# Text order on three engines for the last four pairs of the first half, the scheduler's order ahead of them

## The chip, the cores and the metric

The kernel runs on one core of one Trainium2 chip. The metric is the device time of one execution in microseconds (us). The engines are TensorE (PE in the profile, with its weight loads as PEld), VectorE (DVE), ScalarE (ACT), GpSimd (POOL) and SyncE (SP); SP issues most of the DMAs.

## What is computed

One block of an encoder on a sequence of 2048 tokens with 1024 features, in float32. All projections come out of one large product with the input weights; an attention branch and a short convolution branch are gated, projected, added and projected once more.

```python
h = rmsnorm(x, norm_g[l])
proj = jnp.einsum('bsd,de->bse', h, w_in[l])
q, k, v, z_att, gb, gc, u, z_conv, g_att, g_conv = jnp.split(proj, IN_SPLITS, axis=-1)
att = chunked_rel_attention(q.reshape(...), k.reshape(...), v.reshape(...), rel_bias[l])
y_att = jnp.einsum('bsc,cd->bsd', att * jax.nn.silu(z_att), w_att_out[l])
vconv = causal_depthwise_conv(gc * u, conv_w[l], conv_b[l])
y_conv = jnp.einsum('bsc,cd->bsd', gb * vconv * jax.nn.silu(z_conv), w_conv_out[l])
m = jax.nn.sigmoid(g_att) * y_att + jax.nn.sigmoid(g_conv) * y_conv
x = x + jnp.einsum('bsd,de->bse', m, w_out[l])
return rmsnorm(x, final_norm_g)
```

## The kernel before

**Halves, pairs, items.** The 2048 tokens are worked in two halves of 1024. For each half the input projection is done in 24 pairs of column tiles (`NPAIR`), `names` gives their order; places 0 to 23 of `names` are the first half, 24 to 47 the second. A "pair" below is a place in `names`. Pairs 0 to 2 of the first half are done in a plain way in an opening stage. From pair 3 on, a pair's 2 by 2 block product is done by seven products instead of eight, with numbers 1, 2, 6, 5, 7, 4, 3 in this order (`ORDER`). One such product is called an **item** here. The list `seq` holds all items, and items are counted from 0 at the first product of pair 3: pair 3 is items 0 to 6, pair 9 is items 42 to 48, pair 18 is items 105 to 111. Pairs 22 and 23 are woven into each other (`ending`), items 133 to 146: items 136, 137, 138, 140, 142, 144 and 146 belong to pair 23. Pairs 24 and 25, the first two of the second half, are woven as well (`beginning`), items 147 to 160.

**One item on TensorE.** `passes` (L135 to L137) makes 12 matmuls of 128x512: four row blocks, each as weight-high by operand-high, weight-high by operand-low, weight-low by operand-high. So the third matmul of an item is the first that needs the low part of its weight. Each item writes one PSUM bank `ps_d` out of three, which VectorE (L746, L750, L753, L757 and L758, L762, L766) or, for product 1, ScalarE (L742) reads before the third item after it can start.

**One item's weight.** `operand` (L375) is called two items ahead in the first half. It forms the weight where the product needs a sum (L390 to L392, and L396 for product 7, on VectorE), then ScalarE casts the high part (L122) and VectorE subtracts to get the low part (L123). "W46" below is this split for item 46. The weight tile `wc` comes from a ring of four, so W46 also waits until item 42 is done and until the store of item 42's weight to DRAM (L399, on SP, kept for the second half) has read it.

**What else runs there.** The evacuated sums go on by kind of pair: gates are passed through tanh on ScalarE (L404), q and k are split (L410 cast, L411 subtraction), v is transposed on TensorE (L433) and split (L440, L441), z gets a tanh on ScalarE (L453) and a product on VectorE (L454), the convolution pairs run L472 to L498. During pairs 8 to 21 `norm_steps` prepares the second half's input (squares L293, a chain of small VectorE instructions L72 to L85, scaling L304, differences L335).

**The second half's operands.** During pair 23 each item is followed by one step of `operand_steps` (L348), which makes the operands of the second half for that product in four blocks j. A step splits each block into high and low (cast L128 on ScalarE, subtraction L129 on VectorE). For products 6, 5 and 4 each block is first changed by VectorE (L354, L360, L356), and the cast and the subtraction follow on that block.

**What sets the order.** Inside `tc.manual_schedule(engines=...)` the named engines' instructions stand in the order of the Python text. Engines not named, and everything outside such a block, stand in the order of the framework's scheduler, which goes by its own estimate of when things become ready. Before, the opening stage (L646) is in text order on PE, DVE and ACT; the items of pairs 3 to 25 are in text order on PE and ACT, with DVE left to the scheduler, up to the close at L785; behind that all is the scheduler's.

Of the kernel before, what the change touches and what calls it, by code (L numbers as in the profile page):

```python
# [36 lines left out]
NPAIR = 24  # L37
# [3 lines left out]
def block_kernel(ctx, tc, xb, xt, wp_in, wy, wo, bias, ng, fg, cw, cb, out):  # L41
# [328 lines left out]
    def load_raw(p, n):  # L370
        r = ww.tile([P, 2, 4, P], F32, tag="w", name="wraw")
        raws[p, n] = r
        nc.sync.dma_start(r, wp_in[p % NPAIR, n])
# [270 lines left out]
    engines = {mybir.EngineType.PE, mybir.EngineType.DVE, mybir.EngineType.Activation}  # L644
# [53 lines left out]
        for fn in late:  # L698
            fn()
    manual = ExitStack()  # L700
    manual.enter_context(tc.manual_schedule(engines=engines - {mybir.EngineType.DVE}))
    x1 = None
    nbias = 0
    att = None
# [5 lines left out]
    for s, (p, i) in enumerate(seq):  # L710
        half = p // NPAIR
        n = names.index(p)
        if half == 0 and i == 1 and n + 1 < NPAIR:
            for k in range(2):
                load_raw(names[n + 1], k)
        elif i == 1 and n in (NPAIR, *range(NPAIR + 2, NPAIR + 1 + PLAIN)):
            for k in range(2):
                load_raw(names[max(n, NPAIR + 1) + 1], k)
# [278 lines left out]
```

## Time and profile before

| | us |
|---|---|
| median of 3 runs | 1581.42 |
| lowest, highest of the 3 | 1577.53, 1582.02 |
| the profiled execution's own time | 1571.1 |
| its span, first to last instruction | 1569.3 |
| PE, DVE, ACT busy | 1522.1, 1045.3, 682.6 |
| DMA, mean over the span | 251 GB/s |

Durations below come from the profiled execution. In the views that are quoted further down, a row of the timeline has the start, the duration, engine, line, operation, tile written from tiles read, and in brackets the idle time of the engine just before it and what ended it. A row of the windows view has, for a stretch of time, the busy us of PE, PEld, DVE, ACT and POOL with the count of instructions, then the granted TensorE clock, the DMA engines' busy share and the GB/s. Ends of matmuls are modelled, so distances between starts of matmuls are the better measure. "Item 46" and the like are not in the rows; the items were counted off along PE's rows.

### The profile page before, as it was taken

Reading aid. Unit: us, or ns where it says so; the run is one execution under the profiler, and the core shown is the slowest. Engines: PE = TensorE matmul, PEld = TensorE weight load, DVE = VectorE, ACT = ScalarE, POOL = GpSimd, SP = SyncE. Lnnn points to the kernel's source line nnn. Section 1 sums busy time; section 2 is a strip of 40 time slices with the busy share of each in tenths; the row PEclk is TensorE's granted clock in tenths of the full one; section 3 lists DMA queues with packets and bytes.
Section 4 is the critical chain, followed back from the end, with each engine's and each line's share of the span. In section 5 each row is a group of like instructions: output and inputs, shape, how many; then the busy total and the mean of one; then the engine's idle time right before and its main releaser. Section 6 shows DMA issues by size and latency. Waiting matters only on the chain.

```text
span 1569.3 us, 21720 instructions
## 1 busy us (share of the span) xinstructions
PE 1522.1 (97%) x7396; PEld 1268.2 (81%) x7396; DVE 1045.3 (67%) x2094; ACT 682.6 (43%) x1266; POOL 154.9 (10%) x294
## 2 busy tenths in 40 slices
PE   9899999999998999999999999999999999999997
PEld 6677878888786787888888888888887788888886
DVE  7978779797668653666565455446678786656544
ACT  6353343443335242333344444446666676523211
POOL 0000000000000001111121012012332222000000
PEclk9999999999999999999999999999999899999999
DMA  5287898989996926787899889898967668369231
GB/s 210 79 293 298 309 338 306 371 298 311 332 338 230 318 92 215 222 266 238 295 313 314 303 281 287 270 314 274 294 200 228 203 217 273 124 220 316 67 108 68
DMA packets 161711, 393.65 MB, mean 251 GB/s; under 512 B 20160, under 2 KB 40640, under 8 KB 161600
## 3 DMA queue, kind: packets, MB, share of 16 engines
q1 hardware_dynamic: 131392, 306.25, 56.2%
q0 software_dynamic: 20992, 69.22, 14.0%
q10 hardware_dynamic: 9216, 16.78, 2.9%
q8 instruction: 59, 0.97, 0.3%
q14 instruction: 52, 0.43, 0.1%
HBM read 241.18 MB, written 150.99 MB: 250 GB/s over the span
## 4 chain that ended last, share of the span: by engine, by line
PE 62%; DVE 4%; DMA 2%; ACT 1%; issue 1%; SPq 0%; DVEq 0%; ACTq 0%
PE ps_d L137 13%; PE ps_d L135 13%; PE ps_d L136 13%; PE ps_s L190 4%; PE po L228 4%; PE ps_d L873 3%; PE ps_d L875 3%; PE ps_d L874 3%; PE ps_t L210 3%; DMA wraw<-wy 1%; ACT pr L200 1%; DMA wraw<-wo 0%; DVE ps_s L196 0%; DVE ptl L216 0%; PE vt L433 0%
## 5 line engine op out<-in xcount | busy, mean ns | idle before, releaser
L158 POOL DMA_DIRECT2D q<-q x128 | 66.6, 526 | 710.4 <-DVE wc L123 603.3
L200 ACT ACTIVATE pr<-ps_s,nmax 128x640 f32<-128x640 f32 (+4 forms) x128 | 93.3, 729 | 89.8 <-DVE nmax L196 86.2
L196 DVE CUSTOM_DVE_ANT_0 ps_s<-ps_s,bs 128x640 f32<-128x640 f32 (+4 forms) x128 | 95.4, 745 | 48.1 <-PE ps_s L190 47.5
L215 ACT CAST pth<-ps_t 128x640 fp32r<-128x640 f32 (+4 forms) x128 | 79.8, 623 | 99.9 <-PE ps_t L210 98.5
L202 ACT ACTIVATE pr<-pr,rs 128x640 f32<-128x640 f32 (+4 forms) x128 | 97.7, 763 | 24.2 <-DVE rs L201 24.2
L190 PE MATMUL ps_s<-kk,q 128*128 128x320 f32 (+1 forms) x448 | 99.5, 336 | 8.5 <-ACT pr L200 8.3
L122 ACT CAST wc<-wraw 128x512 fp32r<-128x512 f32 x120 | 72.9, 619 | 76.5 <-DMA wc<-wc 41.6
L136 PE MATMUL ps_d<-mid,wy 128*128 128x512 f32 x256 | 101.4, 396 | 0.0
L135 PE MATMUL ps_d<-mid,wy 128*128 128x512 f32 x256 | 101.2, 395 | 0.0
L137 PE MATMUL ps_d<-mid,wy 128*128 128x512 f32 x256 | 101.2, 395 | 0.0
L216 DVE TENSOR_TENSOR ptl<-ps_t,pth 128x640 fp32r<-128x640 f32 (+4 forms) x128 | 94.2, 736 | 1.1 <-ACT pth L215 0.8
L123 DVE TENSOR_TENSOR wc<-wraw,wc 128x512 fp32r<-128x512 f32 x120 | 81.1, 688 | 12.5 <-ACT wc L122 11.5
L210 PE MATMUL ps_t<-ident,pr 128*128 128x128 f32 x560 | 84.2, 276 | 1.0 <-DVE ptl L216 0.8
L228 PE MATMUL po<-pth,vv 128*128 128x256 f32 x336 | 80.1, 272 | 2.3 <-ACT pth L215 2.2
L228 PE MATMUL po<-ptl,vv 128*128 128x256 f32 x336 | 78.5, 281 | 0.0
L190 PEld LDWEIGHTS ps_s<-kk,q 128*128 128x128 f32 x448 | 67.9, 191 | 13.0 <-ACT pr L200 12.3
L210 PEld LDWEIGHTS ps_t<-ident,pr 128*128 128x128 f32 x560 | 63.3, 140 | 11.1 <-issue 3.2
L228 PEld LDWEIGHTS po<-pth,vv 128*128 128x128 f32 x336 | 64.3, 191 | 6.8 <-ACT pth L215 3.4
L228 PEld LDWEIGHTS po<-ptl,vv 128*128 128x128 f32 x336 | 64.5, 192 | 2.7
L757 DVE TENSOR_TENSOR c<-v,ps_d 128x512 f32<-128x512 f32 x45 | 30.9, 687 | 48.7 <-PE ps_d L137 46.4
L884 ACT ACTIVATE sq<-y 128x512 f32<-128x512 f32 x32 | 20.2, 631 | 92.1 <-DVE y L879 92.0
L746 DVE TENSOR_TENSOR c<-u,ps_d 128x512 f32<-128x512 f32 x45 | 30.9, 686 | 42.3 <-PE ps_d L137 38.5
(370 smaller groups left out, 4260.0 us busy)
## 6 DMA issues: line engine op xcount, KB each, us to landing
wc<-wc SPq DMA_DIRECT2D x294, 512.0 KB, 4.7
wraw<-wp_in SPq DMA_DIRECT2D x54, 512.0 KB, 6.2
q<-q POOLq DMA_DIRECT2D x128, 128.0 KB, 4.9
gl<-gate SPq DMA_DIRECT2D x64, 256.0 KB, 3.9
mid<-mid SPq DMA_DIRECT2D x64, 256.0 KB, 5.7
bs<-bias POOLq DMA_DIRECT2D x32, 320.0 KB, 7.1
gate<-c ACTq DMA_DIRECT2D x34, 256.0 KB, 4.6
v<-vst SPq DMA_DIRECT2D x64, 128.0 KB, 4.6
```

The costliest lines, as they stand in the source:

```text
L123: nc.vector.tensor_sub(w[:, 1], src, w[:, 0].bitcast(F32))
L135: nc.tensor.matmul(ps, lhsT=w[:, 0, k, :], rhs=rh[:, cs], start=(first and k == 0), stop=False)
L136: nc.tensor.matmul(ps, lhsT=w[:, 0, k, :], rhs=rl[:, cs], start=False, stop=False)
L137: nc.tensor.matmul(ps, lhsT=w[:, 1, k, :], rhs=rh[:, cs], start=False, stop=(last and k == len(rhs) - 1))
L190: nc.tensor.matmul(ps[:, i, :m], lhsT=q[s][:, g * P:(g + 1) * P], rhs=kk[:, k1 - n + i * m:k1 - n + (i + 1) * m], start=(s == 0), stop=(s ...
L196: nc.vector.tensor_tensor_reduce(out=view, in0=view, in1=bv, scale=-0.125, scalar=3.0e38, op0=ALU.add, op1=ALU.min, accum_out=nmax)
L200: nc.scalar.activation(out, view, AF.Exp, bias=nmax, scale=-1.0, accum_out=rs)
L202: nc.scalar.activation(pr[:, :n], pr[:, :n], AF.Identity, scale=rs)
L210: nc.tensor.transpose(out=ps[:, j * P:(j + 1) * P], in_=pr[:, j * P:(j + 1) * P], identity=ident)
L215: nc.scalar.copy(hi[:, js, qs], src)
L216: nc.vector.tensor_sub(lo[:, js, qs], src, hi[:, js, qs].bitcast(F32))
L228: nc.tensor.matmul(ps[:, (g0 + a) * P:(g0 + b) * P], lhsT=vv[:, g0 + j, :], rhs=s[:, j, a * P:b * P], start=(i == 0 and s is pt[0]), stop= ...
```

## The change

The block of text order that began ahead of pair 3 and named PE and ACT is not opened there any more. It is opened at pair 20, and it then names PE, DVE and ACT. It closes where it closed before, behind pair 25.

```diff
     manual = ExitStack()
-    manual.enter_context(tc.manual_schedule(engines=engines - {mybir.EngineType.DVE}))
     x1 = None
...
         n = names.index(p)
+        if n == NPAIR - 4 and i == 1:
+            manual.enter_context(tc.manual_schedule(engines=engines))
         if half == 0 and i == 1 and n + 1 < NPAIR:
```

So pairs 3 to 19 are in the scheduler's order on all engines, and pairs 20 to 25 in text order on three. PE's rows stand in the same order in both programs, and so do POOL's. On ACT 203 of 1156 rows stand elsewhere, all in pairs 3 to 26; on DVE 547 of 2096, all in pairs 3 to 26; on SP 116 of 886, by 14 rows at most. Behind pair 26 the order is the same on every engine. Lines behind L712 are one higher in the changed kernel, and the numbers of tiles are two lower up to pair 20; line numbers in the text are those of the kernel before.

The first place is DVE in pair 23, at the step of `operand_steps` for product 5 (item 140): `t1` is the changed block (L360), `t50l` to `t53l` are the low parts of the four blocks, `wc_4812` is the weight of item 143, `v_4786` the sum that evacuates item 140. Before:

```order
L123 TENSOR_TENSOR wc_4768<-wraw_4524,wc_4768 128x512
L360 TENSOR_TENSOR t1_4788<-xs_1605,xs_1596 128x512
L360 TENSOR_TENSOR t1_4794<-xs_1605,xs_1596 128x512
L360 TENSOR_TENSOR t1_4800<-xs_1605,xs_1596 128x512
L129 TENSOR_TENSOR t50l_4791<-t1_4788,t50h_4790 128x512
L360 TENSOR_TENSOR t1_4806<-xs_1605,xs_1596 128x512
L129 TENSOR_TENSOR t51l_4797<-t1_4794,t51h_4796 128x512
L757 TENSOR_TENSOR c22_4829<-v_4766,ps_d_4815 128x512
L129 TENSOR_TENSOR t52l_4803<-t1_4800,t52h_4802 128x512
L758 TENSOR_TENSOR u_4559<-u_4559,ps_d_4815 128x512
L129 TENSOR_TENSOR t53l_4809<-t1_4806,t53h_4808 128x512
L123 TENSOR_TENSOR wc_4812<-wraw_4323,wc_4812 128x512
```

The same place in the changed kernel:

```order
L754 TENSOR_TENSOR v_4786<-u_4649,ps_d_4772 128x512
L360 TENSOR_TENSOR t1_4788<-xs_1603,xs_1594 128x512
L129 TENSOR_TENSOR t50l_4791<-t1_4788,t50h_4790 128x512
L360 TENSOR_TENSOR t1_4794<-xs_1603,xs_1594 128x512
L129 TENSOR_TENSOR t51l_4797<-t1_4794,t51h_4796 128x512
L360 TENSOR_TENSOR t1_4800<-xs_1603,xs_1594 128x512
L129 TENSOR_TENSOR t52l_4803<-t1_4800,t52h_4802 128x512
L360 TENSOR_TENSOR t1_4806<-xs_1603,xs_1594 128x512
L129 TENSOR_TENSOR t53l_4809<-t1_4806,t53h_4808 128x512
L123 TENSOR_TENSOR wc_4812<-wraw_4323,wc_4812 128x512
```

Each L360 now stands directly ahead of the subtraction of the same block, which reads the cast that ACT makes of it, and nothing stands between them. The steps for product 6 (L354) and product 4 (L356) stand the same way.

The second place is ACT in pair 9: `wc_2328` before and `wc_2326` in the change are the weight of item 46, `c11_2324` and `c11_2322` the first sum of the gate. Before:

```order
L404 ACTIVATE c11_2324<-c11_2324 128x512
L405 DMA gate0_5_0_175<-c11_2324 128x512
L122 CAST wc_2328<-wraw_2080 128x512
```

In the changed kernel (L743 is the evacuation of item 42):

```order
L743 COPY u_2295<-ps_d_2278 128x512
L122 CAST wc_2326<-wraw_2078 128x512
L404 ACTIVATE c11_2322<-c11_2322 128x512
```

The cast for item 46 moved from behind the gate's tanh to ahead of it, directly behind the evacuation of item 42. On DVE its other half (L123) moved 20 rows forward, ahead of the chain of small instructions L84 to L78.

The third place is DVE in pair 18: `wc_3896` and `wc_3894` are the weight of item 110, L757 and L758 evacuate item 109. Before:

```order
L757 TENSOR_TENSOR c22_3935<-v_3916,ps_d_3921 128x512
L758 TENSOR_TENSOR u_3850<-u_3850,ps_d_3921 128x512
L123 TENSOR_TENSOR wc_3896<-wraw_3654,wc_3896 128x512
L123 TENSOR_TENSOR wc_3918<-wraw_3652,wc_3918 128x512
L411 TENSOR_TENSOR c22_3935<-c22_3935,hi_3938 128x512
```

In the changed kernel:

```order
L123 TENSOR_TENSOR wc_3894<-wraw_3652,wc_3894 128x512
L758 TENSOR_TENSOR c22_3933<-v_3914,ps_d_3919 128x512
L759 TENSOR_TENSOR u_3848<-u_3848,ps_d_3919 128x512
L411 TENSOR_TENSOR c22_3933<-c22_3933,hi_3936 128x512
L123 TENSOR_TENSOR wc_3916<-wraw_3650,wc_3916 128x512
```

The split for item 110 moved ahead of the evacuation of item 109; the split for item 111 moved behind the split of the k tile (L411).

## The prediction

> **What bounds the kernel now.** I read the page first, then who TensorE waits for, then where in time, then the stretch that the change touches.
>
> ```profile
> span 1569.3 us, 21720 instructions
> PE 1522.1 (97%) x7396; PEld 1268.2 (81%) x7396; DVE 1045.3 (67%) x2094; ACT 682.6 (43%) x1266; POOL 154.9 (10%) x294
> ...
> PE 62%; DVE 4%; DMA 2%; ACT 1%; issue 1%; SPq 0%; DVEq 0%; ACTq 0%
> ```
>
> TensorE sets the pace: busy 97%, and 62% of the chain that ended last. Its order is the same in both programs, so only its waits can change. The view of waits for PE:
>
> ```profile
> PE ps_d L137 <- DVE wc L123: 12.4, 10, 2.9
> ...
> PE ps_d L135 <- ACT wc L122: 3.1, 2, 2.4
> ...
> PE ps_d L135 <- DVE v L753: 0.8, 1, 0.8
> ```
>
> Ten waits for a weight's low part (12.4 us), two for its high part (3.1 us), one for a PSUM bank that VectorE had not read yet. Where they are, by PE's timeline:
>
> ```profile
> 210.49 0.50 PE L135 MATMUL ps_d<-t20h,wc 128*128 128x512 f32 x1 [0.71 <-ACT wc L122]
> 221.78 0.67 PE L135 MATMUL ps_d<-t70h,wc 128*128 128x512 f32 x1 [2.43 <-ACT wc L122]
> 402.33 0.50 PE L137 MATMUL ps_d<-t40h,wc 128*128 128x512 f32 x1 [1.53 <-DVE wc L123]
> 423.19 0.50 PE L137 MATMUL ps_d<-t40h,wc 128*128 128x512 f32 x1 [1.53 <-DVE wc L123]
> 492.45 0.50 PE L137 MATMUL ps_d<-t50h,wc 128*128 128x512 f32 x1 [2.30 <-DVE wc L123]
> 497.26 0.50 PE L137 MATMUL ps_d<-t70h,wc 128*128 128x512 f32 x1 [1.65 <-DVE wc L123]
> 504.48 0.50 PE L137 MATMUL ps_d<-t40h,wc 128*128 128x512 f32 x1 [1.48 <-DVE wc L123]
> 513.27 0.50 PE L137 MATMUL ps_d<-t30h,wc 128*128 128x512 f32 x1 [2.94 <-DVE wc L123]
> ```
>
> These are items 43, 46, 110, 117 (scheduler's part of the change) and 140, 141, 143, 145 (its text part). The other low-part waits are small: 12.4 less the six listed (11.43) leaves 0.97 us in four. Starts of matmuls show the whole loss:
>
> ```profile
> 90.97 0.39 PE L135 MATMUL ps_d<-t10h,wc 128*128 128x512 f32 x1
> ...
> 289.83 0.39 PE L135 MATMUL ps_d<-t10h,wc 128*128 128x512 f32 x1
> ...
> 308.87 0.39 PE L135 MATMUL ps_d<-t10h,wc 128*128 128x512 f32 x1
> ...
> 428.32 0.39 PE L135 MATMUL ps_d<-t10h,wc 128*128 128x512 f32 x1
> ...
> 521.15 0.39 PE L135 MATMUL ps_d<-t20h,wc 128*128 128x512 f32 x1
> ```
>
> Pair 13 runs undisturbed: 308.87 - 289.83 = 19.04 us, 2.72 an item. Pairs 3 to 19 take 428.32 - 90.97 = 337.35 us against 17 x 19.04 = 323.7, so at most **13.7 us** can be gained there.
>
> **First part: pairs 3 to 19, now the scheduler's order on ACT too.** In the old order a cast L122 sat behind ScalarE instructions that wait for something else.
>
> ```profile
> 219.31 0.68 DVE L746 TENSOR_TENSOR c<-u,ps_d 128x512 f32<-128x512 f32 x1
> ...
> 212.99 0.58 ACT L742 COPY u<-ps_d 128x512 f32<-128x512 f32 x1
> ...
> 220.08 0.63 ACT L404 ACTIVATE c<-c 128x512 f32<-128x512 f32 x1 [4.76 <-DVE c L746]
> ...
> 221.11 0.62 ACT L122 CAST wc<-wraw 128x512 fp32r<-128x512 f32 x1 [0.40 <-ACT c L404]
> ```
>
> For item 46 the cast (221.11) waited behind the tanh, which waited 4.76 us for L746, which stood behind the chain of small VectorE rows. In the change it follows the copy of 212.99, so it can run near 213.5, 6 us before item 46 wants it. What is late next there is item 43's bank, read by that same L746: about 0.5 us of wait. The old wait cost 2.43 us and a slower clock behind it:
>
> ```profile
> 220.00:225.00 5.00, 3.22 (x8) 2.39 (x9) 2.58 (x4) 2.39 (x4) 0.00 (x0) 0.69 1.03 408
> ...
> 510.00:515.00 5.00, 2.06 (x9) 1.42 (x8) 5.00 (x10) 2.34 (x5) 0.00 (x0) 1.00 0.96 339
> ```
>
> The granted clock fell to 0.69 of full speed over these 5 us, 0.31 x 5 = 1.6 us lost. So item 46 gives back 2.43 + 1.6 - 0.5 = 3.5. Item 43's weight moves forward by 3 rows on ACT and 7 on DVE: 0.71 idle plus some 0.4 of restart, 1.1. The small waits' weights (items 16, 22, 58, 85) move forward 5 to 10 rows on DVE: 0.97 plus about 0.27 of restart each, 2.0.
>
> ```profile
> 400.38 0.69 DVE L757 TENSOR_TENSOR c<-v,ps_d 128x512 f32<-128x512 f32 x1 [2.03 <-DMA q<-c]
> ...
> 401.59 1.28 DVE L123 TENSOR_TENSOR wc<-wraw,wc 128x512 fp32r<-128x512 f32 x2
> ...
> 397.20 0.62 ACT L122 CAST wc<-wraw 128x512 fp32r<-128x512 f32 x1 [3.11 <-DMA wc<-wc]
> ```
>
> Item 110's cast was done at 397.82, yet its split stood behind L757 and ran at 401.59, while VectorE had idled 2.03 us. In the change it stands ahead: the wait goes, 1.53 + 0.27 = 1.8. Item 117 moves the wrong way: its cast and split now stand behind a k tile's split.
>
> ```profile
> 421.97 0.62 ACT L410 CAST hi<-c 128x512 fp32r<-128x512 f32 x1 [0.92 <-DVE c L757]
> ```
>
> The cast then starts near 422.5, the split ends near 423.85 instead of 423.14: 0.7 more. Sum: 3.5 + 1.1 + 2.0 + 1.8 - 0.7 = 7.7. Against it stands the DMA, which holds weights back through the ring of four:
>
> ```profile
> 91.00:428.00 337.00, 329.69 (x1436) 268.59 (x1435) 264.60 (x472) 130.13 (x238) 0.00 (x0) 0.99 0.89 324
> ```
>
> At a busy share of 0.89 stores can land later than an earlier cast would like. The bounds are no gain at all and the whole 13.7; I take **-7.5**, near the sum, since of the eight listed waits none is put down to a DMA. VectorE (264.60 of 337) and ScalarE (130.13) have room for the rows that moved back; what they delay (gates, k and q tiles, stores) is read only in the second half. SP's stores and loads change places by 14 rows at most, which I cost at nothing: no weight or input block is wanted sooner than several items later.
>
> **Second part: pairs 20 to 25, text order on VectorE.** Here VectorE, not TensorE, is short:
>
> ```profile
> 482.68 0.69 DVE L129 TENSOR_TENSOR t10l<-xs,t10h 128x512 fp32r<-128x512 f32 x1 [1.55 <-ACT t10h L128]
> ...
> 482.60:518.60 36.00, 35.63 (x60) 1.00 0.58 214
> ...
> 519.00:557.00 38.00, 38.00 (x170) 31.46 (x169) 18.41 (x30) 10.70 (x19) 0.00 (x0) 1.00 0.79 274
> ```
>
> From 482.6 to 518.6 it is busy 35.63 of 36.00 us, 60 instructions at 0.60 us, and TensorE's four waits (8.37 us) lie in it. Text order brings the splits forward: items 140, 141, 143 and 145 by 6, 3, 2 and 4 rows. But it also puts each changed block directly ahead of its own subtraction, with ScalarE's cast between. The opening stage, already in text order, shows what that costs:
>
> ```profile
> 78.56 0.69 DVE L360 TENSOR_TENSOR t<-xs 128x512 f32<-128x512 f32 x1
> 79.98 0.69 DVE L129 TENSOR_TENSOR t51l<-t,t51h 128x512 fp32r<-128x512 f32 x1 [0.74 <-ACT t51h L128]
> 80.59 0.68 DVE L360 TENSOR_TENSOR t<-xs 128x512 f32<-128x512 f32 x1
> ...
> 79.33 0.62 ACT L128 CAST t51h<-t 128x512 fp32r<-128x512 f32 x1 [1.42 <-DVE t L360]
> ```
>
> L360 at 78.56, the cast at 79.33, the subtraction at 79.98, the next L360 at 80.59: 2.03 us a block instead of two packed rows, 1.20. That is 0.83 lost a block, and there are 4 blocks in each of the steps for products 6, 5 and 4: 12 x 0.83 = 10.0. Two more such round trips come with L396, now directly ahead of the weights of items 141 and 142: 1.7. Products with silu (sum on VectorE, tanh on ScalarE, product on VectorE) are five in the chain; by the next rows the product follows its sum by 1.45, so 0.85 is lost where nothing lies between (three times) and 0.25 where L758 does (twice): 3.0.
>
> ```profile
> 203.09 0.69 DVE L757 TENSOR_TENSOR c<-v,ps_d 128x512 f32<-128x512 f32 x1
> 203.69 0.68 DVE L758 TENSOR_TENSOR u<-u,ps_d 128x512 f32<-128x512 f32 x1
> 204.54 0.69 DVE L454 SCALAR_TENSOR_TENSOR sz<-sz,c 128x512 f32<-128x512 f32 x1 [0.16 <-ACT sz L453]
> ```
>
> From the first subtraction of pair 23 (482.68) to the evacuation of item 145 the new order has 62 VectorE rows: 62 x 0.60 = 37.2, plus 10.0 + 1.7 + 3.0 = 51.9. L390 to L392 of item 138's weight stand later, so the chain starts some 0.4 later, at 483.1, and ends at 535.0. No row of the chain waits for TensorE, which is far ahead of it; so it is the bound. Along it TensorE waits about 1 us at item 140, 8 at 141 (behind product 6's step and L396), 6 at 143 (behind product 5's step) and 2 at 145. Then comes a wait that was not there: items 145, 146, 147 hold the three banks, item 148 needs item 145's, and that evacuation now stands behind product 4's step. Item 148 starts at 535.0 instead of 521.15: **+13.9**. Slow clock behind the earlier waits is absorbed, VectorE being later; behind the last one (5 to 6 us) it is not, 1.6 by the row of 220 to 225: **+15.5**. Lower bound: with packed rows the chain is 37.2, no loss; upper: two spans of slow clock and another 1.6. I take the sum, since all its rows are of the same instructions. Pairs 24 and 25 hold no further waits: their operands stand ahead, weights 161 to 165 keep two items' lead, and VectorE is busy only 18.41 of 38 us there. Everything behind keeps its order and shifts whole.
>
> The Trainium skill, page "TensorE: Matmul & The Clock Gate", section "What's actually happening", halves the clock after an idle window of about 3.4 us. Here 2.43 us of wait was followed by 0.69, and 2.94 us at 513.27 by 1.00, so the trace bears it out only loosely. By that rule item 46's slow stretch would not belong to its wait, and my estimate would be 1.6 higher, 1591.0.
>
> **Sum.** -7.5 + 15.5 = +8.0. The profiled execution (1571.1) would be 1579.1. It lies 10.3 below the median of the runs, 1581.42; I add the change to the median: **1589.4**.
>
> **Rivals.**
> *The first part gains nothing*: earlier casts stop on the ring until stores land. For it: 3.11 us of wait for the store at 397.20. Against: the waits at items 46 and 110 came from rows ahead, with the cast possible earlier. 1581.42 + 15.5 = 1596.9. Chance 0.16.
> *No difference*: the first part gives 10.9 (13.7 less item 117's and transposes' 2.8), and the last bank's wait passes without slow clock, 13.9: 1584.4. Chance 0.22.
> *Faster*: the weights come earlier by their rows, 6, 3, 2, 4 x 0.60, taking 2.30 + 1.65 + 1.2 + 2.4 = 7.5 us of the waits in pairs 22 and 23, and the first part 7.5: 1566.4. It decides where VectorE finds the casts done, under 0.60 us behind the changed block; against it the 0.74 of wait at 79.98. Chance 0.10.
> That the change does not do what it says is out: the order of rows shows it.
>
> **Chances.** My forecast, a loss of 5 to 12 us: 0.52; with the first rival slower has 0.68, same 0.22, faster 0.10. A measurement of this kernel tells about 0.3%, 4.7 us, from none. The range, 1578 to 1600, takes in both nearer rivals and their errors, and leaves the faster one out.
>
> **What would show it.** L129 t50l to t53l 2.03 us apart on VectorE with idle for ACT t50h; PE waits of 5 us or more at items 141 and 143 and for a bank (L766) at item 148; item 148 some 106.7 us behind pair 20's start, now 521.15 - 428.32 = 92.8; no wait at item 46 and 110, and pairs 3 to 19 in some 330 us instead of 337.35. Wrong would be: subtractions packed at 0.6, or a first part that is no shorter.

## The result, and the profile after

| | before | after |
|---|---|---|
| median of 18 runs each, us | 1577.26 | 1584.03 |
| lowest and highest, us | 1567.24 to 1582.02 | 1579.87 to 1589.09 |
| profiled execution, its own time and span, us | 1571.1, 1569.3 | 1585.07, 1583.3 |

The ratio of after to before, taken from the means of the runs, is 1.0052, 95% interval [1.0038, 1.0065]: about 8.2 us slower (0.0052 x 1577.26); the medians lie 6.8 us apart. Foretold were +8.0 us and 1589.4 us. The level came out 5.4 us lower than foretold: 4.2 us because the kernel before came out lower over 18 runs than over its first three, and 1.2 because the medians lie 6.8 and not 8.0 us apart.

The profiled execution of after is 14.0 us longer in its span. Only part of that belongs to the change, as the starts of items show (in these rows lines behind L712 are one higher than in the kernel before). PE's timeline of the kernel after, at items 0, 119 (start of pair 20), 127, 141, 143, 147 and 148:

```profile
92.59 0.39 PE L135 MATMUL ps_d<-t10h,wc 128*128 128x512 f32 x1
...
419.85 0.39 PE L135 MATMUL ps_d<-t10h,wc 128*128 128x512 f32 x1
...
444.38 0.50 PE L135 MATMUL ps_d<-t20h,wc 128*128 128x512 f32 x1 [1.20 <-ACT u L743]
...
495.69 0.79 PE L135 MATMUL ps_d<-t70h,wc 128*128 128x512 f32 x1 [7.46 <-ACT wc L122]
...
507.64 0.79 PE L135 MATMUL ps_d<-t40h,wc 128*128 128x512 f32 x1 [4.76 <-ACT wc L122]
...
522.85 0.47 PE L135 MATMUL ps_d<-t10h,wc 128*128 128x512 f32 x1 [1.44 <-DMA wc<-wc]
529.50 0.77 PE L135 MATMUL ps_d<-t20h,wc 128*128 128x512 f32 x1 [3.65 <-DVE v L767]
```

Item 0 starts 1.6 us later (92.59, 90.97 before), before the change begins. Pairs 3 to 19 take 419.85 - 92.59 = 327.26 us, **10.1 less** than before (337.35). From pair 20 to item 148 it is 529.50 - 419.85 = 109.65 us, **16.8 more** than before (92.83). Item 150 starts at 536.66 (526.59 before), 1.7 more through slow matmuls behind the wait at 148, and from there to item 167 both kernels keep the same distance. So the changed stretch costs -10.1 + 16.8 + 1.7 = +8.4 us, and the rest of the 14.0 lies in front of it (1.6) and behind item 167 (3.9), where the order of every engine is the same. One profiled execution stands behind each of these figures: the order of before takes 336.47 us for pairs 3 to 19 in second_part_only, and that of after 328.73 in first_part_only (table below), so such a difference is known to 1 or 2 us.

The page and the view of waits for PE of the kernel after, to be held against those of before:

```profile
span 1583.3 us, 21716 instructions
PE 1521.0 (96%) x7396; PEld 1270.0 (80%) x7396; DVE 1045.8 (66%) x2094; ACT 686.2 (43%) x1266; POOL 154.8 (10%) x294
...
PE 56%; DMA 5%; DVE 4%; ACT 2%; issue 1%; SPq 0%; DVEq 0%; ACTq 0%
```

```profile
PE ps_d L135 <- ACT wc L122: 14.8, 4, 7.5
PE ps_p L135 <- DVE c L607: 9.3, 3, 4.6
PE ps_d L135 <- DVE v L767: 3.6, 1, 3.6
PE ps_d L135 <- ACT u L743: 2.4, 2, 1.2
...
PE ps_d L137 <- DVE wc L123: 0.4, 1, 0.4
```

The engines' work is nearly unchanged. The ten waits for a weight's low part (12.4 us) have become one of 0.4; four waits for a high part (3.1 before, now 14.8) and three for a bank (3.6 and 2.4) have come in their place, with the 1.44 us above for item 147's weight to land. The 9.3 us for L607 (6.3 before) lie in the opening stage, ahead of the change.

VectorE in pair 23 of the kernel after, by its timeline (the first subtraction of the pair, product 5's step, then the end of product 4's step and the evacuation that item 148 waits for):

```profile
477.46 0.69 DVE L129 TENSOR_TENSOR t10l<-xs,t10h 128x512 fp32r<-128x512 f32 x1 [0.31 <-ACT t10h L128]
...
499.57 0.68 DVE L360 TENSOR_TENSOR t<-xs 128x512 f32<-128x512 f32 x1
500.99 0.69 DVE L129 TENSOR_TENSOR t50l<-t,t50h 128x512 fp32r<-128x512 f32 x1 [0.74 <-ACT t50h L128]
501.60 0.69 DVE L360 TENSOR_TENSOR t<-xs 128x512 f32<-128x512 f32 x1
503.03 0.69 DVE L129 TENSOR_TENSOR t51l<-t,t51h 128x512 fp32r<-128x512 f32 x1 [0.74 <-ACT t51h L128]
...
528.16 0.69 DVE L129 TENSOR_TENSOR t43l<-xs,t43h 128x512 fp32r<-128x512 f32 x1 [0.74 <-ACT t43h L128]
528.77 0.68 DVE L767 TENSOR_TENSOR v<-v,ps_d 128x512 f32<-128x512 f32 x1
```

A block takes 2.03 us (501.60 - 499.57), 0.74 of it idle for ScalarE's cast. L767 follows product 4's step without a gap, and item 148 (529.50) follows L767.

### The profile page after: what moved, and what is told of

The parts are those of the page before. It is cut to its first block, busy times and chain, and to the rows that moved or that the text cites. A ratio compares the mean times of both kernels' runs of the same rounds, so it can differ in the third digit from the quotient of the medians.

```text
span 1583.3 us, 21716 instructions
## 1 busy us (share of the span) xinstructions
PE 1521.0 (96%) x7396; PEld 1270.0 (80%) x7396; DVE 1045.8 (66%) x2094; ACT 686.2 (43%) x1266; POOL 154.8 (10%) x294
## 4 chain that ended last, share of the span: by engine, by line
PE 56%; DMA 5%; DVE 4%; ACT 2%; issue 1%; SPq 0%; DVEq 0%; ACTq 0%
PE ps_d L135 12%; PE ps_d L137 12%; PE ps_d L136 12%; PE po L228 4%; PE ps_s L190 4%; PE ps_d L876 3%; PE ps_d L875 3%; PE ps_d L874 3%; PE ps_t L210 3%; DMA wraw<-wo 2%; DMA wraw<-wy 1%; DMA wc<-wc 1%; DVE ps_s L196 1%; ACT pr L200 1%; DMA vv<-v 0%
## 5 line engine op out<-in xcount | busy, mean ns | idle before, releaser
L123 DVE TENSOR_TENSOR wc<-wraw,wc 128x512 fp32r<-128x512 f32 x120 | 82.3, 688 | 22.6 <-ACT wc L122 22.5
L190 PEld LDWEIGHTS ps_s<-kk,q 128*128 128x128 f32 x448 | 67.9, 191 | 12.9 <-ACT pr L200 12.4
L210 PEld LDWEIGHTS ps_t<-ident,pr 128*128 128x128 f32 x560 | 63.5, 141 | 10.9 <-issue 3.1
L758 DVE TENSOR_TENSOR c<-v,ps_d 128x512 f32<-128x512 f32 x45 | 30.9, 686 | 48.8 <-PE ps_d L137 48.8
L754 DVE TENSOR_TENSOR v<-u,ps_d 128x512 f32<-128x512 f32 x45 | 30.9, 686 | 48.3 <-PE ps_d L137 46.1
```

Source lines behind the costliest of these rows:

```text
L123: nc.vector.tensor_sub(w[:, 1], src, w[:, 0].bitcast(F32))
L190: nc.tensor.matmul(ps[:, i, :m], lhsT=q[s][:, g * P:(g + 1) * P], rhs=kk[:, k1 - n + i * m:k1 - n + (i + 1) * m], start=(s == 0), stop=(s ...
L210: nc.tensor.transpose(out=ps[:, j * P:(j + 1) * P], in_=pr[:, j * P:(j + 1) * P], identity=ident)
```

## The experiments

Twelve kernels ran, in three groups, each with runs of the kernel before on the same chip (medians 1576.34, 1575.34 and 1576.82 us, 25 to 34 runs). "Stretch 1" is from item 0 to pair 20, "stretch 2" from pair 20 to item 148, both from PE's starts in the profiled execution.

| kernel | median us (runs) | ratio to before, 95% | stretch 1 | stretch 2 |
|---|---|---|---|---|
| before | | | 337.35 | 92.83 |
| after | 1584.03 (18) | 1.0052 [1.0038, 1.0065] | 327.26 | 109.65 |
| first_part_only | 1567.34 (12) | 0.9948 [0.9927, 0.9969] | 328.73 | 95.04 |
| second_part_only | 1592.22 (6) | 1.0108 [1.0072, 1.0143] | 336.47 | 109.70 |
| changed_blocks_first | 1572.1 (12) | 0.9970 [0.9951, 0.9990] | 327.28 | 99.74 |
| no_block | 1568.35 (12) | 0.9956 [0.9934, 0.9977] | 327.25 | 93.86 |
| late_steps | 1581.39 (12) | 1.0035 [1.0013, 1.0057] | 328.77 | 105.76 |
| sums_early | 1578.34 (12) | 1.0010 [0.9990, 1.0030] | 328.81 | 105.38 |
| three_edits | 1567.96 (12) | 0.9951 [0.9927, 0.9975] | 327.73 | 94.80 |
| first_part_late_steps | 1567.75 (11) | 0.9944 [0.9922, 0.9965] | 327.25 | 95.06 |
| weights_earlier | 1587.8 (6) | 1.0067 [1.0045, 1.0089] | 328.65 | 109.40 |
| three_edits_weights | 1567.16 (8) | 0.9942 [0.9920, 0.9964] | 327.25 | 94.74 |
| first_part_weights | 1572.4 (12) | 0.9968 [0.9947, 0.9989] | 328.81 | 95.55 |
| before_gate_later | 1576.96 (12) | 1.0007 [0.9984, 1.0029] | 336.25 | 94.85 |

### Each part alone

first_part_only, against the change:

```diff
         if n == NPAIR - 4 and i == 1:
-            manual.enter_context(tc.manual_schedule(engines=engines))
+            manual.enter_context(tc.manual_schedule(engines=engines - {mybir.EngineType.DVE}))
```

> Pairs 3 to 19 as in the change, pairs 20 to 25 as before (text order on PE and ACT, VectorE left to the scheduler). Theory: the change is a gain in pairs 3 to 19 (7.5 us predicted, 10 read from the two traces) and a loss behind pair 20, and the two are independent. Then this is faster than before by 7 to 11 us, ratio 0.993 to 0.996, with no wait at items 46 and 110 and the waits at 140, 141, 143, 145 as before. Rival (casts only stop on the ring until stores land, the trace's gain is chance): ratio 0.999 to 1.001.

second_part_only, against the kernel before (whose block from pair 3 on stays):

```diff
+        if n == NPAIR - 4 and i == 1:
+            manual.close()
+            manual.enter_context(tc.manual_schedule(engines=engines))
```

> Pairs 3 to 19 as before, pairs 20 to 25 in text order on PE, ACT and VectorE. Theory: slower than before by 15 to 19 us, ratio 1.0095 to 1.012, item 148 some 107 to 111 us behind pair 20's start (92.8 before). Rival (the loss needs the scheduler's order ahead of it, through DMA or tile slots): less than half of that, under 1.006.

Measured 0.9948 and 1.0108: -8.2 us and +17.0 us. Their product is 1.0055, within the interval of the change, so within these intervals the parts add up and neither hides the other. The rival by which the first part gains nothing falls, and so does the one by which the second is free or helps. TensorE in pair 23 of first_part_only, by its timeline, waits as the kernel before did:

```profile
486.36 0.50 PE L137 MATMUL ps_d<-t50h,wc 128*128 128x512 f32 x1 [2.28 <-DVE wc L123]
...
508.24 0.79 PE L137 MATMUL ps_d<-t30h,wc 128*128 128x512 f32 x1 [2.93 <-DVE wc L123]
```

### The round trips

changed_blocks_first is the change, with the second half's steps for products 6, 5 and 4 written so that VectorE changes all four blocks before it splits the first:

```diff
+            if half and i in (6, 5, 4):
+                made = []
+                for j in range(4):
...
+                for j in range(4):
+                    split_t(half, i, j, made[j])
+                yield i
+                continue
```

> As the change, but in the second half's operand steps for products 6, 5 and 4 all four changed blocks stand first in the text and the four casts and subtractions behind them. Theory (12 round trips VectorE-ScalarE-VectorE at 0.83 us each make the chain long): VectorE's chain in pair 23 is 10 us shorter, waits at items 141 and 143 shrink by 3.3 and some 5 us, the bank wait at 148 goes; 8 to 12 us less than the change, ratio to before 0.997 to 1.000. Rival (VectorE's plain volume, or the place of the evacuations, sets it): within 3 us of the change, ratio 1.003 to 1.007.

Measured 0.9970, which is 12.9 us less than the change (0.0082 x 1576.34), a little more than the 8 to 12 us expected. VectorE's timeline of this kernel at product 5's step and at the evacuation of item 145 (L363 is the change of a block, L360 above, and L784 is L767 above):

```profile
495.99 2.49 DVE L363 TENSOR_TENSOR t<-xs 128x512 f32<-128x512 f32 x4
498.40 0.68 DVE L129 TENSOR_TENSOR t50l<-t,t50h 128x512 fp32r<-128x512 f32 x1
499.00 0.69 DVE L129 TENSOR_TENSOR t51l<-t,t51h 128x512 fp32r<-128x512 f32 x1
...
518.55 0.69 DVE L784 TENSOR_TENSOR v<-v,ps_d 128x512 f32<-128x512 f32 x1
```

The same eight rows follow each other at 0.60 us, and the idle time for the casts is gone. Counted from pair 20's start (419.55) the evacuation of item 145 comes 99.0 us in, 108.9 in the change (528.77 - 419.85): 9.9 us less, against the 12 x 0.83 = 10.0 of the prediction. TensorE's waits shrink with it, 7.46 to 4.14 us at item 141, 4.76 to 0.46 at 143, 3.65 to 0.71 at 148, and so do slow stretches behind them: from item 148 to 150 it is 5.57 us instead of 7.16, another 1.6. The trace so shows 11.5 of the 12.9 us, and the interval of the runs is some 3 us to each side.

### No text order at all

no_block leaves the block out altogether:

```diff
-        if n == NPAIR - 4 and i == 1:
-            manual.enter_context(tc.manual_schedule(engines=engines))
```

> No text order anywhere behind the opening stage: pairs 20 to 25 in the scheduler's order on all engines too. Theory: pairs 3 to 19 as in the change, and behind pair 20 VectorE's volume in pair 23 (60 rows at 0.60 us) still bounds, so about as first_part_only: ratio 0.991 to 0.996. Rival (ScalarE's text order is what holds pairs 22 and 23 up): the waits at items 140 to 145 go too, ratio under 0.990.

Measured 0.9956; stretch 2 takes 93.86 us, 15.8 less than in the change. first_part_only, which keeps text order on TensorE and ScalarE, takes 95.04 us, so it is VectorE's text order that costs there.

### The bank of item 148, and the banks of items 127 and 134

late_steps moves the steps for products 4 and 3 behind items 148 and 150:

```diff
-            assert next(turned) == i
+            if i not in (4, 3):
+                assert next(turned) == i
...
+        if n in (NPAIR, NPAIR + 1) and i == 2:
+            next(turned)
```

> The change, but the steps of operand_steps for products 4 and 3 stand behind the second products of pairs 24 and 25 (items 148 and 150) instead of in pair 23; nothing else differs, and DVE and ACT rows move only there. Theory: item 148 waits in the change (3.65 us for L767, then 1.7 us of slow clock) only because the evacuation of item 145 stands behind product 4's step of 8.1 us; with that step moved the wait is gone and the 1.4 us for item 147's weight stay: item 150 comes 5 us earlier than in the change, ratio to before 1.002 (1.001 to 1.003) instead of 1.005. Rival: the loss sits in the chain as a whole and comes back at the moved steps or at the weights behind them: item 160 no earlier than in the change, ratio 1.005.

Measured 1.0035 [1.0013, 1.0057]; the expected 1.002 lies in the interval, but so does 1.005, so the trace has to decide. PE at items 147, 148 and 152, by the timeline of late_steps:

```profile
525.10 0.47 PE L135 MATMUL ps_d<-t10h,wc 128*128 128x512 f32 x1 [1.05 <-DMA wc<-wc]
...
528.24 0.47 PE L135 MATMUL ps_d<-t20h,wc 128*128 128x512 f32 x1 [0.18 <-DMA wc<-wc]
...
540.20 0.50 PE L135 MATMUL ps_d<-t60h,wc 128*128 128x512 f32 x1 [0.79 <-ACT u L743]
```

The bank wait of 3.65 us at item 148 and the slow matmuls behind it are gone; 0.79 us comes back at item 152, behind the moved step. From pair 20's start, item 150 comes 5.5 us earlier than in the change (533.80 - 422.48 against 536.66 - 419.85) and item 160 4.2 us earlier (562.30 - 422.48 = 139.82 against 563.87 - 419.85 = 144.02). The term is shown, with a quarter of it given back.

sums_early forms the sums for products 6 and 7 of pairs 20 to 23 one item earlier in the text than their cast (L390 to L392 and L396, moved into a function `form`):

```diff
+        if half == 0 and n >= NPAIR - 4 and seq[nw][0] < NPAIR and seq[nw][1] in (6, 7):
+            form(*seq[nw])
```

> The change, but in pairs 20 to 23 the sums for products 6 and 7 (L390 to L392, L396) stand one item earlier in the text than their cast. Theory: the waits of 1.20 us at items 127 and 134 come from the weight of items 128 and 135, whose cast and subtraction wait for sums that stand behind the evacuation of items 125 and 132, with the reader of the bank behind them; they go (2 x 1.44), and the two round trips of L396 in pair 23 go too (1.45): item 148 comes some 4 us earlier, ratio 1.0025 (1.001 to 1.004). Rival: those banks wait for the transposed tiles' own round trips (L440, L441), whatever stands ahead: waits at items 127 and 134 of over 1 us stay, ratio 1.004 to 1.005.

Measured 1.0010 [0.9990, 1.0030]. The wait at item 127 fell from 1.20 to 0.24 us and that at item 134 is gone; stretch 2 is 4.3 us shorter, which is the 0.96 us of the wait at item 127, the 1.44 by which item 134 was late and the 2 x 0.73 of the round trips of L396, to 0.4 us. What held those banks shows in the ScalarE and VectorE rows of the change, by their timelines:

```profile
441.76 0.62 ACT L122 CAST wc<-s 128x512 fp32r<-128x512 f32 x1 [5.26 <-DVE s L391]
442.28 0.36 ACT L440 CAST vst<-vt 128x256 fp32r<-128x256 f32 x1
443.47 0.37 ACT L440 CAST vst<-vt 128x256 fp32r<-128x256 f32 x1 [0.82 <-DVE vst L441]
443.74 0.59 ACT L743 COPY u<-ps_d 128x512 f32<-128x512 f32 x1
```

```profile
439.57 0.69 DVE L767 TENSOR_TENSOR v<-v,ps_d 128x512 f32<-128x512 f32 x1 [0.73 <-PE ps_d L137]
440.18 0.68 DVE L390 TENSOR_TENSOR s<-wraw 128x512 f32<-128x512 f32 x1
440.90 0.69 DVE L391 TENSOR_TENSOR s<-s,wraw 128x512 f32<-128x512 f32 x1
...
443.87 0.42 DVE L441 TENSOR_TENSOR vst<-vt,vst 128x256 fp32r<-128x256 f32 x1 [0.44 <-ACT vst L440]
```

In text order L390 waits behind the evacuation of item 125 (L767, which waits for TensorE), ScalarE stands 5.26 us at the cast of item 128's weight, and everything behind that cast, the split of the transposed tile (L440, L441) and the copy L743, is late. Which of the two item 127 waited for is not settled: L743 ends at 444.33, the second L441 at 444.29, item 127 starts at 444.38. Both stand behind the same cast.

### Is it the chain, or the place of the weights' splits?

weights_earlier forms the weights one item earlier in pairs 22 and 23:

```diff
-        ahead = 3 if half else 2
+        ahead = 3 if half or n >= NPAIR - 2 else 2
```

> The change, but in pairs 22 and 23 a weight is formed three items ahead in the text instead of two, so its cast and split stand ahead of one step of operand_steps more. Theory: VectorE's chain of rows and round trips is the bound of pair 23; its rows and round trips are the same, so the waits at items 141 and 143 shrink and come back at item 148, whose bank stands at the end of the chain: item 148 within 2 us of 109.65 us behind the start of pair 20, ratio 1.005 (1.003 to 1.006). Rival: the place of the weights' splits is the bound, not the chain: the waits go and do not come back, item 148 5 us or more earlier, ratio 1.002 or less.

Measured 1.0067 [1.0045, 1.0089], and item 148 starts 109.40 us behind pair 20, against 109.65. PE's timeline of this kernel at items 142, 144, 146 and 148:

```profile
500.08 0.77 PE L135 MATMUL ps_d<-t70h,wc 128*128 128x512 f32 x1 [7.86 <-DVE v L754]
...
511.21 0.47 PE L135 MATMUL ps_d<-t40h,wc 128*128 128x512 f32 x1 [2.57 <-ACT sz L453]
...
518.26 0.47 PE L135 MATMUL ps_d<-t30h,wc 128*128 128x512 f32 x1 [1.35 <-DVE u L763]
...
530.37 0.80 PE L135 MATMUL ps_d<-t20h,wc 128*128 128x512 f32 x1 [6.43 <-DVE v L767]
```

The waits for weights became waits for banks, and the last of them grew from 3.65 to 6.43 us. Items 136 to 148 take 55.76 us, 56.63 in the change, so no gain is hidden by a loss ahead of pair 23. The rival falls: VectorE's chain sets the end of pair 23, and where TensorE waits along it is indifferent.

### How far down it goes

three_edits puts the last three edits (changed blocks first, late steps, early sums) into the change together.

> The change with all three edits: changed blocks first (0.9970 alone), steps for products 4 and 3 late, sums early. Theory (VectorE's chain in text order, each term by itself): from 0.9970 the bank waits at items 127 and 134 (2.9 us), L396 (1.5) and what is left at item 148 (0.9) go: 0.9935 (0.992 to 0.995), under the 0.9948 of the scheduler's order. Rival: the volume of VectorE in pair 23 bounds whatever the order: 0.9955 to 0.997.

Measured 0.9951 [0.9927, 0.9975], between the two expectations. Stretch 2 takes 94.80 us, as good as the scheduler's own order (95.04 in first_part_only): with the three edits text order costs nothing there. three_edits_weights adds the line of weights_earlier.

> The three edits (0.9951) and the weights of pairs 22 and 23 three items ahead. Theory: without the round trips and with product 4's step behind item 148 the chain ends early enough that nothing is due at its end, and what is left is the place of the weights' splits (3.0 us at item 141, 3.5 in item 141, 1.4 at 145): 5 to 7 us less, ratio 0.991 (0.990 to 0.993). Rival: VectorE's volume up to item 145 is still the bound: 0.994 to 0.996.

Measured 0.9942 [0.9920, 0.9964], not told apart from three_edits; stretch 2 is 94.74 against 94.80. The time is what the rival said, but the trace has a gain and a loss in it. Items 136 to 148 take 40.81 us, 3.3 less than in three_edits (44.14), with waits for banks (the longest 3.02 us for VectorE's evacuation, at item 142) in place of the waits for weights. Items 133 to 135, ahead of pair 23, take 12.56 us, 3.3 more (9.26), with new waits of 1.68 and 1.09 us at items 134 and 135. The same on top of first_part_only:

> The first part alone (VectorE the scheduler's: 0.9948), and the weights of pairs 22 and 23 three items ahead. In first_part_late_steps the four waits of items 140 to 145 (2.46, 1.68, 1.63, 3.09 us) stayed to 0.02 us although rows of product 4 had left the stretch, so theory: they come from the place of each split among the rows, and go: 6 to 9 us less, ratio 0.990 (0.989 to 0.992). Rival: VectorE's volume (34.7 of 36 us busy) is the bound and the loss comes back as a wait for a bank at items 147 and 148: 0.994 to 0.995.

Measured 0.9968 [0.9947, 0.9989], stretch 2 95.55 us against 95.04: the expected gain did not come in time. The trace again has both parts. In pair 23 the waits shrank from 8.0 us in all to 5.3 (1.61 in item 142, 1.21 in 144, 2.46 in 146), and items 136 to 148 take 40.43 us, 4.5 less than in first_part_only (44.91). Items 133 to 135 take 14.20 us, 4.9 more (9.26). ScalarE's and PE's rows around item 134, by the timelines:

```profile
465.94 0.62 ACT L122 CAST wc<-wraw 128x512 fp32r<-128x512 f32 x1 [6.15 <-DMA wraw<-wp_in]
...
467.92 0.59 ACT L743 COPY u<-ps_d 128x512 f32<-128x512 f32 x1
...
468.56 0.53 PE L135 MATMUL ps_d<-t20h,wc 128*128 128x512 f32 x1 [3.10 <-ACT u L743]
```

Formed one item earlier, the first weight of pair 23 is wanted before its load has landed; ScalarE, in text order, waits 6.15 us for it at the cast, and the copy that item 134 waits for by the profile stands behind that cast. In three_edits_weights the same cast waits 1.98 us for the load. So in both kernels the earlier splits took 3 to 5 us off pair 23 and lost as much ahead of it. Slow clock (last section) is in these figures: two slow stretches of 3.41 us in pair 23 became none here and one in three_edits_weights, and here one came at items 133 to 135. Whether VectorE's volume is the bound that is left there is not shown by these two kernels. no_block comes nearest to it: from the first subtraction of pair 23 to the start of item 148 its VectorE has 64 rows in 38.5 us and no idle time. A kernel that forms these weights earlier and also loads them earlier did not run.

The fourth of this group, first_part_late_steps, puts the edit of late_steps on top of first_part_only:

> The first part alone (the block opened at pair 20 with PE and ACT, VectorE the scheduler's: 0.9948), with the steps for products 4 and 3 behind items 148 and 150. Theory: the waits at items 140 to 145 are VectorE's volume in pair 23 (35.6 of 36 us busy, 60 instructions); 16 rows of 60 leave it, 9.6 us, so items 143 and 145 lose their waits (1.8 and 4.6): ratio 0.991 (0.989 to 0.993). Rival: they come from the order of the rows: waits of the same size, 0.9948.

Measured 0.9944 [0.9922, 0.9965], not told apart from first_part_only, and the four waits in pair 23 stayed: by the timeline they are 2.31, 1.51, 1.47 and 2.92 us (2.28, 1.28, 1.50 and 2.93 in first_part_only), not the 2.46, 1.68, 1.63 and 3.09 that the expectation above gives. This does not speak against volume: in first_part_only's VectorE rows t40l to t43l (the first at 509.90) stand behind the split that item 145 waits for (507.50) anyway, so the edit took none of them from ahead of the waits. The expectation had overlooked that.

### Item 46 in the kernel before

before_gate_later keeps the block of the kernel before, and writes the gates' tanh one item later:

```diff
+            def go():
+                nc.scalar.activation(t, t, AF.Tanh, scale=0.5)
+                nc.scalar.dma_start(gate_d[i][d][g], t)
+            defer(0, go) if d >= PLAIN else go()
```

> The kernel before, but the gates' tanh (L404) of pairs 3 to 15 is written one item later, so that on ScalarE the cast of the next weight stands ahead of it; the block stays as it was. Theory: item 46 waits (2.43 us, then 1.6 us of slow clock) because its cast stands behind the tanh that waits for L746; the wait goes: 3 to 4 us less, ratio 0.9977 (0.997 to 0.9985), about half of what the first part gives. Rival: what is late there is VectorE (L746 and the small rows), and the wait stays or moves to the bank of item 43: ratio 0.9995 to 1.0005.

Measured 1.0007 [0.9984, 1.0029]: the expected gain did not come in time. ScalarE, VectorE and PE rows of this kernel around item 46 (its cast, the evacuation of item 43, the tanh, its first matmul), from the timeline; its lines are one (L404) or two (L746) higher than before:

```profile
219.93 0.61 ACT L122 CAST wc<-wraw 128x512 fp32r<-128x512 f32 x1
...
224.32 0.68 DVE L748 TENSOR_TENSOR c<-u,ps_d 128x512 f32<-128x512 f32 x1
...
225.10 0.63 ACT L405 ACTIVATE c<-c 128x512 f32<-128x512 f32 x1 [4.56 <-DVE ry L78]
...
225.15 0.47 PE L135 MATMUL ps_d<-t70h,wc 128*128 128x512 f32 x1 [1.09 <-DVE ry L78]
```

The cast of item 46 is done 4.6 us before the item starts, as foretold, and the slow clock behind the wait is gone; but the item still waits 1.09 us, for the bank that L748 reads at 224.32 behind the small rows (the profile names L78, the small row behind L748, here and at the tanh, which reads what L748 writes). So ScalarE's order was one part of that wait and VectorE's order the other. Pair 9 takes 22.17 us (24.75 before, 19.04 in the change). Part of the gain was lost at items 5 (1.8 us, 0.3 before) and 64 (0.9, none before), which now wait for the low part of their weight: stretch 1 is only 1.1 us shorter than in before, and 0.2 shorter than in second_part_only, which has the same order there.

## Why the prediction came out right

**The sum was better than its parts.** Foretold were -7.5 and +15.5; the trace shows -10.1 and +18.5, the separate runs -8.2 and +17.0. Both terms were too small, by 2.6 and 3.0 us in the trace and by 0.7 and 1.5 in the separate runs, and the errors cancelled: that the sum came within 0.2 us of the ratio's 8.2 is luck.

**First part: mechanism right, size too small.** Pair 9 gave 5.7 us (24.75 to 19.04) where items 46 and 43 were to give 4.6. The step that failed is the 0.5 us of wait left for item 43's bank: L746 starts 7.5 us into the pair instead of 12.4, ahead of more of the small rows, which start earlier themselves, so nothing was left. The other 0.6 us is spread over both items. Items 16, 22, 58 and 85 gave 2.2 (2.0 foretold), item 110 1.8 (1.8). Item 117 became 0.8 worse (0.7 foretold), and 2.2 in first_part_only, where the clock was slow behind it. Not counted were items 5, 37, 79 and 92, whose delays of 0.1 to 0.4 us with restart made another 1.1; I had taken the small waits from the rows that show an idle time of their own and not from the distances of starts. The cut from 7.7 to 7.5 for the DMA was needless: no wait in that stretch is put down to one.

**Second part: the chain was right to 0.1 us, its start was not.** From the first subtraction of pair 23 to item 148 it took 529.50 - 477.46 = 52.0 us; 51.9 were foretold, and changed_blocks_first took 9.9 us out of it where 10.0 were put in. The smaller terms fit too: the rows show 1.7 us lost at the two L396 (1.7 foretold) and 2.9 at the five products with silu (3.0). But the chain started 57.6 us behind pair 20 (477.46 - 419.85) instead of 54.8 (483.1 - 428.32). The step that failed is "the chain starts some 0.4 later": I had looked at where L390 to L392 moved on VectorE for one weight in pair 23, and not at who stands behind the cast that reads them on ScalarE in pairs 20 and 21. There text order cost 2 x 1.44 us of TensorE's time, and sums_early took most of it back. That is the 2.9 us by which +13.9 for item 148 was too small (16.8).

**Waits along the chain.** Foretold about 1, 8, 6, 2 and 5 to 6 us at items 140, 141, 143, 145 and 148; found 1.0, 7.5, 4.8, none and 3.65, and 1.44 at item 147 for a weight's load, which had not been foretold. Their places and sizes do not matter, as weights_earlier shows. Slow clock behind the last wait cost 1.7 us (1.6 foretold). The other level that the prediction names, 1591.0, has item 46's slow stretch stay without its wait; it went with the wait, and items 45 and 46 take 2.72 us each in after.

**The rivals.** That the first part gains nothing is excluded by first_part_only, no difference by the interval of the result, since the slow clock behind the last wait did come; its larger first part, 10.9 us, was nearer to the trace's 10.1 than my 7.5. The faster case was to decide where VectorE finds the casts done; it found each one 0.74 us late, in all twelve blocks.

**Versions that beat both kernels.** first_part_only, no_block, three_edits, first_part_late_steps and three_edits_weights lie at 0.9942 to 0.9956, all with intervals below 1 and none told apart from the others; changed_blocks_first and first_part_weights, at 0.9970 and 0.9968, lie below 1 too. The simplest is no_block: the change without its block.

## What to carry to other kernels

Text order on an in-order engine is priced by its round trips: where a row reads what another engine makes of the row just ahead of it, add what each costs (0.83 us here, 0.74 of it seen as idle time), and write the independent rows first. Where the engine that is put in order is already the short one, sum its rows and round trips: here that gave the length of the chain to 0.1 us, and moving the waits along it gained nothing. For each instruction that moves behind a late one, look on the next engine too, at what stands behind its reader. When an edit gains nothing, look ahead of the stretch that it was made for: here 4.5 us gained in pair 23 were lost at the three items before it.

## What the runs showed of the hardware

The clock behind a short wait was not the same from one execution to the next. Item 117 waits 1.95 us for the same cast in after and in first_part_only, with the same rows around it. The windows behind it, of after and of first_part_only:

```profile
414.00:419.00 5.00, 4.92 (x21) 3.76 (x22) 2.86 (x6) 1.86 (x4) 0.00 (x0) 1.00 0.82 300
```

```profile
414.00:419.00 5.00, 3.95 (x10) 2.82 (x11) 2.26 (x4) 1.98 (x4) 0.00 (x0) 0.66 0.80 316
```

The granted clock (third figure from the end) is 1.00 in one and 0.66 in the other, and that is why stretch 1 takes 327.3 us in some executions and 328.7 in others. Behind the waits of 7.46, 4.76 and 3.65 us in after it fell each time. The Trainium skill, page "TensorE: Matmul & The Clock Gate", section "What's actually happening", has the clock fall after at least one idle window of about 3.4 us, and says that this window is free-running. That the same wait is followed by either clock agrees with a free-running window, and so do the long waits; that a wait of 1.95 us can bring the slow clock at all does not agree with a whole window of idle time.

The windows view shows what decided here. In all fourteen profiles the slow stretches are 3.41 us long or a multiple, at a clock of 0.50, so that one costs 1.7 us, and within a profile they start on one grid of 3.41 us: in after at 492.02, 505.67 and 529.57, which is 4 and 11 times 3.41 us apart from the first. Cut along that grid, first before around the waits at items 46 and 145, then first_part_only and after around the wait at item 117:

```profile
218.53:221.94 3.41, 0.98 (x5) 0.52 (x4) 2.26 (x7) 1.46 (x3) 0.00 (x0) 1.00 1.05 412
221.94:225.35 3.41, 3.41 (x9) 2.48 (x10) 1.71 (x3) 0.92 (x2) 0.00 (x0) 0.50 0.97 384
508.66:512.07 3.41, 1.67 (x8) 0.90 (x6) 3.41 (x7) 3.06 (x6) 0.00 (x0) 1.00 0.88 279
512.07:515.48 3.41, 2.21 (x10) 1.80 (x11) 3.41 (x6) 0.62 (x1) 0.00 (x0) 1.00 1.00 399
```

```profile
412.16:415.57 3.41, 1.46 (x6) 0.67 (x5) 3.23 (x6) 1.77 (x4) 0.00 (x0) 1.00 0.92 356
415.57:418.98 3.41, 3.35 (x9) 2.51 (x9) 0.78 (x2) 0.41 (x1) 0.00 (x0) 0.50 0.80 319
```

```profile
410.10:413.51 3.41, 1.87 (x9) 1.21 (x7) 2.59 (x5) 0.79 (x2) 0.00 (x0) 1.00 1.04 411
413.51:416.92 3.41, 2.93 (x12) 2.12 (x13) 1.76 (x3) 1.39 (x3) 0.00 (x0) 1.00 0.73 294
```

Where one stretch of the grid held 2.43 or 1.95 us of wait (TensorE busy 0.98 and 1.46 us), the next was at 0.50. Where the grid cut the wait, so that 1.74 of 2.94 us or 1.54 of 1.95 us lay in one stretch (busy 1.67 and 1.87), the next stayed at 1.00. Counted from TensorE's idle times over the stretches at full clock in the fourteen profiles (from 30 us on, without the end of each execution), all 80 with 1.85 us of idle time or more were followed by a slow one, and of 6083 with 1.75 us or less only one. Stretch 2 depends on this too: before, with no slow stretch in it, takes 92.83 us, and first_part_only, with two, 95.04. The opening stage, the same rows in all fourteen kernels, also ended at different times: item 0 started between 90.65 and 93.88 us in their profiled executions.
